# Down's weight sums by DMA into two residual quarters, and whole SwiGLU tiles loaded for its tile sums

## The chip, the cores and the metric

One core of a Trainium2 chip runs the kernel in a single launch. The metric is the device time of one execution in microseconds (us). The kernel before takes 1428.65 us, the median of 3 runs (1428.42 to 1428.69). Line numbers (L121) are those of the kernel before, whose profile is shown.

## The reference

The reference is one layer of a transformer-like encoder in fp32: batch 1, sequence 256, width 2048, SwiGLU width 5632. Four mixers, cross-attention on 256 memory rows, and a SwiGLU block follow each other, each with an RMS norm and a residual sum; a last norm ends it.

```python
x = x + mix @ w_out[l]
x = x + cross_attention(rms_norm(x, norm_g[l, 1]), mem_n, w_xq[l], w_xkv[l], w_xo[l])
x = x + swiglu(rms_norm(x, norm_g[l, 2]), w_gate_up[l], w_down[l])
return rms_norm(x, final_norm_g)

def swiglu(h, w_gate_up, w_down):
    gate, up = jnp.split(h @ w_gate_up, 2, axis=-1)
    return (jax.nn.silu(gate) * up) @ w_down
```

The change concerns the last two matrix products: `gate_up` (256 x 2048 by 2048 x 11264) and `down` (256 x 5632 by 5632 x 2048). They take the time from about 700 us to the end.

## The kernel before

**Products in fp32.** Each operand is split into a rounded high part and a residual low part, and a product is three matmuls with the weights moving: high by high, high by low, low by high (`part`, L472 to L474). The activations lie still, as tiles of 128 rows (k) x 256 (sequence), high and low side by side in 512 columns. A matmul has a 128 x 128 still tile and 512 moving columns.

**The weight stream.** All weights come as slabs of 128 x 2048 fp32 (1 MB) in the order in which the program uses them. `_load` (L105 to L129) issues a slab's DMA on SP's queue into one of three `raw` buffers. `_plain` (L147) turns it into two halves of 1024 columns: ScalarE casts the high part (L166), VectorE subtracts it for the residual (L167). The halves lie in a ring of three pairs of buffers `wh` and `wl`, and pools of stages that have ended are lent to the ring for a while, so a cast waits until TensorE has done with an earlier half.

**Paired slabs.** Two k-tiles and two column blocks together are a 2 x 2 product of blocks. A plain slab ("N" in a plan) takes eight block products, 24 matmuls. A paired slab takes seven by a Strassen-like scheme, 21 matmuls: it needs sums of weight blocks and sums of activation blocks. `_sums` (L171 to L199) makes its four parts of 1024, 512, 1024 and 1024 columns (L178, L179), and the weight sums by VectorE adds of 128 x 512 (L189). `combine` (L477 to L494) makes the activation sums of two tiles, in small adds, and splits them into high and low (L338 and L322). `paired_rows` (L502) walks through a plan, takes the parts as they come, and adds seven products into PSUM banks.

**Where the weight sums come from.** In gate_up a paired slab is "summed": the first sum is made by DMA in a quarter of `res`, the residual rows (four buffers of 128 x 1024, `res0` to `res3`), which are parked in DRAM meanwhile (`leave`). Three slabs ahead (`SUMS`), SP loads 256 KB (L114), ScalarE copies it beside itself (L119), and POOL issues a DMA of 512 KB that adds to what is there (L121). SP then loads only 1536 columns of the slab itself (L124), and VectorE has two adds instead of four. Down's paired slabs are not summed before: all four adds are VectorE's.

**gate_up** (L1100 to L1233) makes 11 blocks of 512 gate and 512 up columns, eight slabs each; blocks 1 to 10 follow the plans in `GROUPS`. A block's result is transposed by VectorE (L598) and stored to DRAM as `hidden` by POOL (`store_turned`, L594). It is loaded back in tiles of 128 x 256 by POOL (`load_turned`, L602, issued at L605) into `tmp` and split by ScalarE and VectorE (`split`, L330 and L322) into the slots `f[k]`, k = 0 to 43 (`fetch`, L1140). 22 of them are fetched during gate_up, the other 22 from the tenth block on, six loads ahead. Slots lie in buffers of earlier stages (`act`, `f`, `z`).

**down** (L1235 to L1310) makes the 2048 columns in two passes of 1024, 22 slabs each, by the plans in `PASSES`; the second pass leaves three slabs to `down_end`. Pair i sums the tiles f[2i] and f[2i+1]; `combine` there first adds the high and low parts of each tile back together (two adds of 128 x 256), since the slots hold nothing else. `mixed` and `done` add the results into `res`, which is reloaded from DRAM in four DMAs of 512 KB right after gate_up (L1230).

**What sets the order.** Every engine runs its queue in program order, and the program is written in TensorE's order. Side work (loads of tiles, `combine`) are generators in `Background` (L243): a planner counts TensorE's time and what VectorE owes, and steps a generator when its yielded pause has passed; `ready` and `before` step it in any case where a tile or sum is needed. `keep` and `keep_place` pin the places of instructions in their engine's queue, and from the end of the attention on the casts and residual splits of the stream keep their order.

Of the kernel before, what the change touches and what calls it, by code (L numbers as in the profile page):

```python
# [24 lines left out]
R = 256  # L25
# [15 lines left out]

LATE = 12

GATE_UP = 1920 // 16 + 8
# [5 lines left out]
PAIRED = {a + i for a, plan in [(GATE_UP + 8 * j, GROUPS[j % len(GROUPS)]) for j in range(10)] + [(DOWN, PASSES[0]), (DOWN + 22, PASSES[1])]  # L50
          for i, x in enumerate(plan) if x in "Ss"}
AHEAD = (-3, -3)

SUMS = [{GATE_UP + 8 * j + i + a: GATE_UP + 8 * j + i for j in range(10) for i, x in enumerate(GROUPS[j % len(GROUPS)]) if x == "S"}
        for a in AHEAD]

SUMMED = {GATE_UP + 8 * j + i for j in range(10) for i, x in enumerate(GROUPS[j % len(GROUPS)]) if x == "S"}

# [18 lines left out]
class Stream:  # L77


    def __init__(self, tc, pools, W, bg):  # L80
# [13 lines left out]
        self.two = []  # L94
        self.begun = []

# [8 lines left out]
    def _load(self, n):  # L105
# [4 lines left out]
        self.raw = slot[0].tile([P, 2048], F32, name="raw", tag="raw")  # L110
        if n // 16 in SUMS[0]:
            t = self.sums[0]
            self.sums.append(self.sums.pop(0))
            nc.sync.dma_start(t[:, 0:512], self.W[SUMS[0][n // 16]][:, 1536:2048])  # L114
            self.begun.append(t)
        if n // 16 in SUMS[1]:
            t = self.begun.pop(0)
            mark = len(nc.cur_bb.bb.instructions)
            nc.scalar.copy(t[:, 512:1024], t[:, 0:512])  # L119
            self.keep(mark)  # L120
            nc.gpsimd.dma_start(t, self.W[SUMS[1][n // 16]][:, 512:1536], accum_op=ALU.add)  # L121
            self.two.append(t)
# [170 lines left out]
class Block:  # L293
# [563 lines left out]
    def whole(self, c):  # L857
        return self.res[c].rearrange("p k r -> p (k r)")

    def leave(self, c):  # L860
        self.nc.sync.dma_start(self.rd[:, c * 1024:(c + 1) * 1024], self.whole(c))
# [238 lines left out]
    def gate_up(self, gp, f, z):  # L1100
# [39 lines left out]
        def fetch(k0, k1, ahead, pause, after=0, slow=False):  # L1140

            m = {}
            for k in range(k0, k1 + ahead):
# [11 lines left out]
                if k >= k0 + ahead:  # L1155
                    while k0 == 0 and k - ahead >= 20 and "free" not in box:
                        yield
# [48 lines left out]
        up(0, ps[1])  # L1206
        early = fetch(0, FT - 22, 2, 2.0, 12, True)
        self.bg.drain(comb)
        for j in range(1, DFF // 512):
            plan = GROUPS[(j - 1) % len(GROUPS)]  # L1210
            if j == 10:
                box["free"] = True
# [22 lines left out]
    def down(self, f, sp):  # L1235
# [8 lines left out]
        u = sp.tile([P, 512], F32, name="u")  # L1244
        sums = [((2 * i, 2 * i + 1), z[i % 8]) for i in range(PASSES[1].count("S"))]
# [41 lines left out]
        def ready(k):  # L1287

            need = min(FT, max(k + 3, FT - 22 + next(asked) * 3 // 4))
            while self.have < need:  # L1290
                self.bg.step(next(e for e in self.bg.q if e[0] is self.fetch))

        for i, plan in enumerate(PASSES):
            n = plan.count("S")
# [13 lines left out]
            if i == 0:  # L1308
# [683 lines left out]
```

## Time and profile before

| What | Value |
|---|---|
| Median of 3 runs | 1428.65 us (1428.42 to 1428.69) |
| Profiled execution | 1428.43 us, span 1426.6 us |
| Mean granted TensorE clock | 0.999 |
| TensorE busy | 1416.5 us, 99% of the span |
| VectorE busy | 1174.3 us, 82% |
| ScalarE busy | 850.2 us, 60% |
| POOL busy | 243.4 us, 17% |
| Moved by DMA | 344.84 MB, 242 GB/s |
| Down starts | about 1186 us |

In the profile, PE is TensorE, DVE is VectorE, ACT is ScalarE, POOL is GpSimd, and SP issues most DMAs. A group's row has the line, the engine, the operation, out<-in with tile names and shapes, the count, the busy time, the mean ns of one, and the idle time before them with what ended it. A timeline's row has the start and duration in us, and in brackets the idle time before it and its releaser. A row of windows has the stretch in us, its length, the busy us (and count) of PE, PE's weight loads, VectorE, ScalarE and POOL, the granted clock, the mean busy share of the DMA engines (a value over 1 comes from overlapping records) and GB/s. A row of DMA issues has the count, KB each, and the median us from issue to landing.

### The profile page before, as it was taken

How to read it: one execution, taken by the hardware profiler on the slowest of the kernel's cores; microseconds unless marked ns; L12 is line 12 of the kernel's file. 1: busy time of each engine (PE TensorE's matmuls, PEld its weight loads, DVE VectorE, ACT ScalarE, POOL GpSimd, SP SyncE). 2: the span in 40 equal slices, each digit the busy share in tenths (PEclk: the TensorE clock that was granted, in tenths of full speed). 3: DMA queues.
4: the chain of work that ended last, by engine and by line, in shares of the span. 5: the costliest groups of instructions: out<-in, count | busy, mean ns of one | idle time of the engine just before them, and what ended most of it. 6: DMA issues, size and time to landing. Idle time of an engine off the chain costs nothing.

```text
span 1426.6 us, 18663 instructions
## 1 busy us (share of the span) xinstructions
PE 1416.5 (99%) x6562; PEld 1176.1 (82%) x6562; DVE 1174.3 (82%) x1782; ACT 850.2 (60%) x1242; POOL 243.4 (17%) x315
## 2 busy tenths in 40 slices
PE   9999999999999999999999999999999999999997
PEld 8888888888888888888888888888888888788886
DVE  6667868787878767677578999999999988989997
ACT  7566665445755555555465676667666665655655
POOL 0000100003212233531331121122211024000000
PEclk9999999999999999999999999999999999999999
DMA  9886554457566797965798999999999898665554
GB/s 356 294 291 250 204 198 174 161 177 232 183 216 215 234 278 249 276 197 188 252 298 257 265 280 283 288 291 260 278 291 273 276 276 242 212 235 179 193 220 148
DMA packets 72462, 344.84 MB, mean 242 GB/s; under 512 B 10894, under 2 KB 12591, under 8 KB 45745
## 3 DMA queue, kind: packets, MB, share of 16 engines
q1 hardware_dynamic: 52976, 285.31, 57.4%
q0 software_dynamic: 18960, 57.69, 17.2%
q8 instruction: 51, 0.84, 0.2%
q10 hardware_dynamic: 432, 0.66, 0.1%
q14 instruction: 43, 0.34, 0.1%
HBM read 321.07 MB, written 22.54 MB: 241 GB/s over the span
## 4 chain that ended last, share of the span: by engine, by line
PE 92%; issue 3%; DVE 2%; DMA 2%; POOL 1%; ACT 0%; SPq 0%; DVEq 0%; ACTq 0%; POOLq 0%
PE pg L472 21%; PE pg L474 21%; PE pg L473 21%; PE pm L473 6%; PE pm L474 6%; PE pm L472 6%; PE pg L420 4%; PE pg L421 2%; PE pm L1445 1%; DMA raw<-in_W 1%; PE pm L1074 1%; DMA tmp<-hidden 1%; POOL tmp L605 1%; PE pm L1045 1%; DVE wl L179 0%
## 5 line engine op out<-in xcount | busy, mean ns | idle before, releaser
L167 DVE TENSOR_TENSOR wl<-raw,wh 128x1024 fp32r<-128x1024 f32 (+1 forms) x395 | 473.7, 1212 | 161.3 <-ACT wh L166 159.4
L166 ACT CAST wh<-raw 128x1024 fp32r<-128x1024 f32 (+1 forms) x395 | 406.4, 1042 | 253.0 <-PE pg L474 189.0
L472 PE MATMUL pg<-wh,act 128*128 128x512 f32 (+1 forms) x1165 | 455.5, 391 | 0.0
L474 PE MATMUL pg<-wh,act 128*128 128x512 f32 (+1 forms) x1165 | 453.9, 390 | 0.5 <-DVE act L322 0.5
L473 PE MATMUL pg<-wl,act 128*128 128x512 f32 (+1 forms) x1165 | 453.6, 389 | 0.2 <-DVE wl L167 0.2
L474 PEld LDWEIGHTS pg<-wh,act 128*128 128x128 f32 x1165 | 218.9, 188 | 47.0 <-DVE act L322 1.1
L472 PEld LDWEIGHTS pg<-wh,act 128*128 128x128 f32 x1165 | 219.0, 188 | 46.8 <-issue 1.5
L473 PEld LDWEIGHTS pg<-wl,act 128*128 128x128 f32 x1165 | 219.0, 188 | 45.1 <-DVE wl L167 0.5
L178 ACT CAST wh<-raw 128x1024 fp32r<-128x1024 f32 (+1 forms) x177 | 161.5, 918 | 158.8 <-DVE raw L189 62.7
L179 DVE TENSOR_TENSOR wl<-raw,wh 128x1024 fp32r<-128x1024 f32 (+1 forms) x177 | 182.7, 1057 | 25.7 <-ACT wh L178 24.3
L473 PE MATMUL pm<-wl,act 128*128 128x512 f32 x290 | 112.9, 389 | 0.2 <-DVE wl L167 0.2
L472 PE MATMUL pm<-wh,act 128*128 128x512 f32 x290 | 112.8, 389 | 0.0
L474 PE MATMUL pm<-wh,act 128*128 128x512 f32 x290 | 112.8, 389 | 0.0
L420 PE MATMUL pg<-act,wh 128*128 128x512 f32 x256 | 90.5, 395 | 0.0
L121 POOL DMA_DIRECT2D res<-in_W x39 | 35.0, 897 | 238.3 <-ACT res L119 211.1
L421 PE MATMUL pg<-act,wl 128*128 128x256 f32 x256 | 71.8, 280 | 0.0
L189 DVE TENSOR_TENSOR raw<-raw 128x512 f32<-128x512 f32 x99 | 68.2, 689 | 1.6
L473 PEld LDWEIGHTS pm<-wl,act 128*128 128x128 f32 x290 | 54.4, 188 | 11.8 <-DVE wl L167 0.5
L474 PEld LDWEIGHTS pm<-wh,act 128*128 128x128 f32 x290 | 54.4, 188 | 11.3
L472 PEld LDWEIGHTS pm<-wh,act 128*128 128x128 f32 x290 | 54.4, 188 | 11.3
L420 PEld LDWEIGHTS pg<-act,wh 128*128 128x128 f32 x256 | 48.1, 188 | 10.5
L178 ACT CAST wh<-res 128x1024 fp32r<-128x1024 f32 x39 | 41.2, 1055 | 14.8 <-PE pg L474 4.1
(376 smaller groups left out, 1933.0 us busy)
## 6 DMA issues: line engine op xcount, KB each, us to landing
raw<-in_W SPq DMA_DIRECT2D x207, 1024.0 KB, 5.5
raw<-in_W SPq DMA_DIRECT2D x39, 768.0 KB, 8.9
res<-in_W POOLq DMA_DIRECT2D x39, 512.0 KB, 9.7
res<-in_W SPq DMA_DIRECT2D x39, 256.0 KB, 4.9
raw<-in_W SPq DMA_DIRECT2D x11, 512.0 KB, 7.1
hidden<-g POOLq DMA_DIRECT2D x22, 256.0 KB, 4.0
tmp<-hidden POOLq DMA_DIRECT2D x44, 128.0 KB, 10.5
features<-tmp POOLq DMA_DIRECT2D x32, 128.0 KB, 4.6
```

Source lines behind the costliest of these rows:

```text
L121: nc.gpsimd.dma_start(t, self.W[SUMS[1][n // 16]][:, 512:1536], accum_op=ALU.add)
L166: nc.scalar.copy(wh[:, a:b], r[:, a:b])
L167: nc.vector.tensor_tensor(out=wl[:, a:b], in0=r[:, a:b], in1=wh[:, a:b].bitcast(F32), op=ALU.subtract)
L178: nc.scalar.copy(wh, src)
L179: nc.vector.tensor_tensor(out=wl, in0=src, in1=wh.bitcast(F32), op=ALU.subtract)
L189: nc.vector.tensor_tensor(out=out, in0=a, in1=b, op=ALU.add)
L420: self.nc.tensor.matmul(p[:, :], wh, slot[:, :], start=start, stop=False)
L421: self.nc.tensor.matmul(p[:, 0:R], wl, slot[:, 0:R], start=False, stop=stop)
L472: self.nc.tensor.matmul(p, hi, wh, start=start, stop=False)
L473: self.nc.tensor.matmul(p, hi, wl, start=False, stop=False)
L474: self.nc.tensor.matmul(p, lo, wh, start=False, stop=stop)
L605: self.nc.gpsimd.dma_start(t.rearrange("p (g t) -> p g t", t=32), src)
```

## The change

- All ten paired blocks of gate_up have the plan "NSSNSSNN"; the tenth was "NSNSNSNN". That is 40 paired slabs instead of 39.
- Down has seven paired slabs in its first pass instead of six, and ten instead of nine in the second. All seven of the first and seven of the second ("S") are now summed by DMA as in gate_up; three ("s") keep the four adds on VectorE.
- Down's sums have only the quarters `res2` and `res3`. `begins` sets at which slab a sum is begun: three slabs ahead, but not before the slab after that of the quarter's last user; the first two are begun six slabs ahead, which is in gate_up. SP's load, ScalarE's copy and POOL's accumulating load are now issued at one place.
- `res0` and `res1` are reloaded after gate_up, `res2` and `res3` in the second pass, two slabs after its last "S".
- `combine` takes, in Down, the whole tiles of a pair from DRAM: POOL loads both (128 KB each) into the two halves of one tile `u`, the generator pauses for 10 us of TensorE's time, and the two adds that joined high and low are left out. The next pair's loads are issued when the adds of the pair before stand in the queue.
- The sums of a pair are forced two slabs ahead of use rather than at the slab itself.
- 20 tiles are fetched during gate_up instead of 22, the rest seven loads ahead instead of six, from the third slab of the last block on instead of the fourth; the rate at which Down asks for them is 5/8 a call instead of 3/4, and more of the first pass's first steps go to the early tiles.

In the built programs, matmuls go from 6450 to 6441, VectorE's two-operand instructions from 1324 to 1301, ScalarE's copies and casts from 956 to 980, SP's DMAs from 371 to 386 and POOL's from 305 to 340.

```diff
-GROUPS = *["NSSNSSNN"] * 9, "NSNSNSNN"
+GROUPS = "NSSNSSNN",
-PASSES = "NNNNNSNNSNNSNSNNSNNSNN", "NSNSNSNSNSNSNSNSNSNNNN"
+PASSES = "NNNNNSNSNNSNSNNSNSNSNN", "NSSNSNSNSNSNSNssNsNNNN"
...
+def begins():
+    at = {}
+    for ns, tiles in (([n for n in sorted(SUMMED) if n < DOWN], 4), ([n for n in sorted(SUMMED) if n >= DOWN], 2)):
+        for i, n in enumerate(ns):
+            a = max(n - 3, ns[i - tiles] + 1) if i >= tiles else n - (3 if tiles > 2 else 6)
+            at[a] = n
+    return at
+SUMS = begins()
...
-    def combine(self, z, a, b):
-        tt, t, u, v, w = self.tt, *(self.tmp() for _ in range(4))
-        for x, y in ((t, a), (u, b)):
-            tt(x, y[:, 0:R].bitcast(F32), y[:, R:512].bitcast(F32), ALU.add)
-        yield SOON
+    def combine(self, z, a, b, whole=None):
+        tt = self.tt
+        if whole:
+            t, u, v, w = *whole, self.tmp(), self.tmp()
+        else:
...
-        early = fetch(0, FT - 22, 2, 2.0, 12, True)
+        early = fetch(0, EARLY, 2, 2.0, 12, True)
...
-                rest = fetch(FT - 22, FT, 6, SOON, slow=True)
+                rest = fetch(EARLY, FT, 7, SOON, slow=True)
...
+                if (j, i) == (10, 4):
+                    self.st.sums = whole[2:]
-                if j == 10 and i > 2:
+                if j == 10 and i > 1:
                     next(rest)
...
-        for c, x in enumerate(whole):
-            nc.sync.dma_start(x, self.rd[:, c * 1024:(c + 1) * 1024])
+        self.fetch_rows((0, 1))
...
         def combined(n):
-            for ks, x in sums[len(made):n]:
-                yield from self.combine(x, *(f[k] for k in ks))
+            whole = [u[:, a:a + R] for a in (0, R)]
+            todo = sums[len(made):n]
+            def load(ks):
+                mark = self.mark()
+                for y, k in zip(whole, ks):
+                    self.load_turned(y, self.ff, k)
+                self.keep_place(mark)
+            load(todo[0][0])
+            yield 10.0
+            for i, (ks, x) in enumerate(todo):
+                yield from self.combine(x, *(f[k] for k in ks), whole)
                 made.append(x)
-                yield 2.0
+                if i + 1 < len(todo):
+                    load(todo[i + 1][0])
+                    yield 10.0
...
-            need = min(FT, max(k + 3, FT - 22 + next(asked) * 3 // 4))
+            need = min(FT, max(k + 3, EARLY + next(asked) * 5 // 8))
...
-            g = self.bg.add(combined(n))
+            g = self.bg.add(combined(n), go=True)
...
-                while plan[j] == "S" and len(made) <= plan[:j].count("S"):
+                while len(made) < sum(x in "Ss" for x in plan[:j + 2]):
                     self.bg.step(next(e for e in self.bg.q if e[0] is g))
+                if i and j == plan.rindex("S") + 2:
+                    self.fetch_rows((2, 3))
...
-                                        () if i else range(2 * n, 2 * n + 8))
+                                        () if i else range(2 * n, EARLY))
```

More of the change, by code (lines that the diff above doesn't have):

```diff
@@ L42 @@
 LATE = 12
+EARLY = 20
 GATE_UP = 1920 // 16 + 8
-GROUPS = *["NSSNSSNN"] * 9, "NSNSNSNN"
+GROUPS = "NSSNSSNN",
 DOWN = GATE_UP + 80
-PASSES = "NNNNNSNNSNNSNSNNSNNSNN", "NSNSNSNSNSNSNSNSNSNNNN"
[L50 to L57, printed above, removed]
+PASSES = "NNNNNSNSNNSNSNNSNSNSNN", "NSSNSNSNSNSNSNssNsNNNN"
+PLANS = [(GATE_UP + 8 * j, GROUPS[j % len(GROUPS)]) for j in range(10)] + [(DOWN, PASSES[0]), (DOWN + 22, PASSES[1])]
+PAIRED, SUMMED = ({a + i for a, plan in PLANS for i, x in enumerate(plan) if x in kinds} for kinds in ("Ss", "S"))
+def begins():
[3 more added lines that the diff above has]
+            a = max(n - 3, ns[i - tiles] + 1) if i >= tiles else n - (3 if tiles > 2 else 6)
+            assert a not in at and a < n, (a, n)
+            at[a] = n
+    return at
+SUMS = begins()
 LAG, OWED, SOON, FAR = 1.3, 0.9, 0.01, 18.0
@@ L110, in _load @@
         self.raw = slot[0].tile([P, 2048], F32, name="raw", tag="raw")
-        if n // 16 in SUMS[0]:
+        if n // 16 in SUMS:
             t = self.sums[0]
             self.sums.append(self.sums.pop(0))
[L114 to L117, printed above, removed]
+            nc.sync.dma_start(t[:, 0:512], self.W[SUMS[n // 16]][:, 1536:2048])
             mark = len(nc.cur_bb.bb.instructions)
@@ L120, in _load @@
             self.keep(mark)
-            nc.gpsimd.dma_start(t, self.W[SUMS[1][n // 16]][:, 512:1536], accum_op=ALU.add)
+            nc.gpsimd.dma_start(t, self.W[SUMS[n // 16]][:, 512:1536], accum_op=ALU.add)
             self.two.append(t)
@@ L475, in part @@
         self.bg.pe(0.68 * wh.shape[1] / 512)
-    def combine(self, z, a, b):
-        tt, t, u, v, w = self.tt, *(self.tmp() for _ in range(4))
-        for x, y in ((t, a), (u, b)):
-            tt(x, y[:, 0:R].bitcast(F32), y[:, R:512].bitcast(F32), ALU.add)
-        yield SOON
+    def combine(self, z, a, b, whole=None):
[3 more added lines that the diff above has]
+        else:
+            t, u, v, w = (self.tmp() for _ in range(4))
+            for x, y in ((t, a), (u, b)):
+                tt(x, y[:, 0:R].bitcast(F32), y[:, R:512].bitcast(F32), ALU.add)
+            yield SOON
         tt(v[:, 0:P], t[:, P:R], u[:, P:R], ALU.subtract)
@@ L858, in whole, with fetch_rows @@
         return self.res[c].rearrange("p k r -> p (k r)")
+    def fetch_rows(self, cs):
+        for c in cs:
+            self.nc.sync.dma_start(self.whole(c), self.rd[:, c * 1024:(c + 1) * 1024])
     def leave(self, c):
@@ L1155, in fetch @@
                 if k >= k0 + ahead:
-                    while k0 == 0 and k - ahead >= 20 and "free" not in box:
-                        yield
                     mark = self.mark()
@@ L1293, in down @@
         for i, plan in enumerate(PASSES):
-            n = plan.count("S")
-            g = self.bg.add(combined(n))
+            n = sum(x in "Ss" for x in plan)
+            g = self.bg.add(combined(n), go=True)
             late = (0, LATE)[i]
```

5 lines of the change are left out of this document (1 added, 4 removed).

## The prediction

> **What bounds the kernel now.** I read the busy shares first, then the stages, then TensorE's own waits. The page:
>
> ```profile
> span 1426.6 us, 18663 instructions
> PE 1416.5 (99%) x6562; PEld 1176.1 (82%) x6562; DVE 1174.3 (82%) x1782; ACT 850.2 (60%) x1242; POOL 243.4 (17%) x315
> ```
>
> PE is busy 99% of the span. The busy time by stage (gate_up's paired blocks, Down's first and second pass, the end):
>
> ```profile
> core 0: us, PE busy (x) PEld busy (x) DVE busy (x) ACT busy (x) POOL busy (x), PEclk, DMA share, GB/s
> 700.00:1186.00 486.00, 486.00 (x2146) 402.43 (x2145) 439.52 (x558) 311.99 (x394) 92.69 (x109) 1.00 0.92 280
> 1186.00:1310.00 124.00, 123.27 (x542) 101.36 (x541) 113.51 (x188) 71.65 (x108) 16.45 (x19) 1.00 0.66 215
> 1310.00:1405.00 95.00, 94.72 (x417) 77.60 (x415) 90.81 (x129) 57.33 (x72) 0.00 (x0) 1.00 0.55 202
> ```
>
> PE is without a gap in gate_up and idle for 1.0 us in both passes of Down, at full granted clock. All that PE waited for from 700 us on, in us, times and longest:
>
> ```profile
> PE pg L474 <- DVE act L322: 0.5, 1, 0.5
> PE pm L472 <- ACT y L338: 0.2, 1, 0.2
> PE pm L473 <- DVE wl L167: 0.2, 1, 0.2
> ```
>
> So each matmul less is worth its own time, and VectorE, though 92% busy in Down's first pass (113.51 of 124), holds PE up for under 1 us. Two places in PE's timeline give the price of a matmul and the two stalls:
>
> ```profile
> 1208.18 0.39 PE L472 MATMUL pg<-wh,z 128*128 128x512 f32 x1
> 1213.62 0.39 PE L472 MATMUL pm<-wh,act 128*128 128x512 f32 x1
> 1215.71 0.47 PE L472 MATMUL pm<-wh,y 128*128 128x512 f32 x1 [0.25 <-ACT y L338]
> 1232.33 0.50 PE L474 MATMUL pg<-wh,act 128*128 128x512 f32 x1 [0.48 <-DVE act L322]
> ```
>
> 1208.18 and 1213.62 are the starts of Down's slabs 4 (plain) and 5 (paired): 24 matmuls in 5.44 us, so 0.227 each, a paired slab of 21 takes 4.76, and Down starts at 1213.62 - 5 x 5.44 = 1186.42.
>
> **The change part by part.** *Removed on PE:* the built kernel has 9 matmuls of 128x512 less (one paired slab more in gate_up and one in each pass, 3 matmuls each): 9 x 0.227 = 2.04 us, all on the path. If the two stalls of 0.25 and 0.48 go too, 2.77. The profiled execution took 1428.43 us (span 1426.6 and 1.8 around it; 0.2 under the median of 1428.65), so 1425.66 is the floor of this change, unless something outside Down moves too.
>
> *Removed on VectorE:* two adds in each of 14 slabs that become summed, and two adds of whole tiles in each of 17 pairs of Down:
>
> ```profile
> L189 DVE TENSOR_TENSOR raw<-raw 128x512 f32<-128x512 f32 x60 | 41.2, 687 | 0.5
> L322 DVE TENSOR_TENSOR tmp<-f 128x256 f32<-128x256 f32 x10 | 4.2, 418 | 0.0
> L322 DVE TENSOR_TENSOR tmp<-tmp 128x128 f32<-128x128 f32 x36 | 9.6, 285 | 0.1
> L179 DVE TENSOR_TENSOR wl<-raw,wh 128x1024 fp32r<-128x1024 f32 x45 | 54.9, 1220 | 6.5 <-ACT wh L178 6.3
> L179 DVE TENSOR_TENSOR wl<-raw,wh 128x512 fp32r<-128x512 f32 x15 | 10.3, 686 | 1.1 <-ACT wh L178 1.1
> ```
>
> That is about 14 x 2 x 0.687 = 19.2 us and 17 x 2 x 0.42 = 14.3 us of an engine for which PE waits under 1 us: worth at most the stalls counted above. If VectorE becomes the bound after a late input, the relief only shortens the recovery.
>
> *Added:* 14 sums by DMA in Down (a load by SP, a copy by ScalarE, an accumulating load by POOL), and two loads of 128 KB per pair by POOL into one tile `u`. Rows of such transfers, with median us to landing, and ScalarE's and POOL's price of issuing:
>
> ```profile
> res<-in_W POOLq DMA_DIRECT2D x39, 512.0 KB, 9.7
> res<-in_W SPq DMA_DIRECT2D x39, 256.0 KB, 4.9
> tmp<-hidden POOLq DMA_DIRECT2D x44, 128.0 KB, 10.5
> L119 ACT COPY res<-res 128x512 f32<-128x512 f32 x39 | 23.9, 614 | 0.0
> L121 POOL DMA_DIRECT2D res<-in_W x39 | 35.0, 897 | 238.3 <-ACT res L119 211.1
> L166 ACT CAST wh<-raw 128x1024 fp32r<-128x1024 f32 x140 | 142.2, 1047 | 30.6 <-PE pg L474 14.2 <-PE pm L474 13.8 <-issue 2.2
> ```
>
> ScalarE's copies (14 x 0.61) fit beside the 58 to 60% of its use in Down (71.65 of 124, 57.33 of 95); POOL has idle time. What can cost are the loads' landings: `u` is one buffer, so a pair's loads can only be issued when the pair before has read it, and the adds that read `u` stand in VectorE's queue in front of the residual splits that PE needs next.
>
> *T1, the first paired slab of Down.* `u` lies where gate_up's last tiles lie, so its first loads wait until the last block's two stores have landed:
>
> ```profile
> 1189.69 1.52 POOL L600 DMA_DIRECT2D hidden<-g  x2 [33.32 <-DVE g L598]
> 1191.20 7.03 POOL L605 DMA_DIRECT2D tmp<-hidden  x8
> 1206.21 1.91 POOL L605 DMA_DIRECT2D tmp<-hidden  x2 [0.36 <-issue]
> hidden<-g POOLq DMA_DIRECT2D x2, 256.0 KB, 4.2
> L605 POOL DMA_DIRECT2D tmp<-hidden x1: 882/882/882, 1207.2 to 1207.2; - x1
> DMA to landing us min/median/max: 11.5/11.5/11.5
> DMA to landing us min/median/max: 5.2/10.7/13.1
> 1195.00:1200.00 5.00, 5.00 (x23) 4.13 (x23) 2.11 (x4) 2.49 (x4) 4.33 (x6) 1.00 1.06 254
> ```
>
> The row with two numbers after x1 is one load: issued at 1207.2, landed 11.5 later; it is the fifteenth from 1191.2 on. The last landing row is that of all 22 loads of this burst. DMA is full there (share 1.06).
>
> In after Down starts 0.68 earlier, at 1185.74; the second store starts at 1190.4 - 0.7 and lands 4.2 later, at 1193.9. POOL then issues, at 0.88 each (7.03 / 8), two loads into `u`, eleven of tiles, and the second pair's two: these are fourteenth and fifteenth, and the last starts at 1206.2 or later. I take 1206.4 and the burst's median of 10.7 to landing rather than 11.5, since 1 MB of residual rows is no longer reloaded at this place: 1217.1. Four adds of 0.285 and the 512-wide split of 0.69 follow: 1218.9. Slab 5 begins at 1185.74 + 5 x 5.44 = 1212.94 and needs that split two products later, at 1214.30: **4.6 late**. VectorE then has 4.4 us of work up to the sum's split (two adds 1.37, splits and tiles 1.83, 1.22), while PE has one product of 0.68: **3.7 more**. T1 = 8.3. If these loads landed in the least time of the row below (4.9), 0; with 13.1, 10.7.
>
> *T2 to T5, later pairs.* The DMA share falls after 1220, and so would the landing:
>
> ```profile
> DMA to landing us min/median/max: 4.9/10.0/13.7
> raw<-in_W SPq DMA_DIRECT2D x21, 1024.0 KB, 6.5
> raw<-in_W SPq DMA_DIRECT2D x29, 1024.0 KB, 5.0
> ```
>
> The first is that of the 22 tile loads between 760 and 1150; the weight loads took 6.5 between 1100 and 1240 and 5.0 between 1250 and 1400, a factor of 0.77. A load alone on its queue (4.9) would take 3.8, the median 7.7 (or 10.0 unchanged); I take L = 6.3, midway between 4.9 and 7.7.
>
> T2: the adds of the fourth pair stand in VectorE ahead of the tile split that slab 9's last step needs. From the end of slab 7 (T): a cast 1.05, a split 1.22, two tile splits 0.84, three adds that free `u` 0.86, POOL's second load starts at T + 4.85, lands at + L; an add, a 512-wide split and the tile's 0.42 make 1.39. Needed at T + 5.44 + 3 x 1.36 + 0.45 = T + 9.97. Late by L - 3.7: **2.6** (0 to 4.5).
>
> T3 to T5: here POOL issues the pair's loads behind the accumulating load of a sum, which waits for its quarter. From the start T of a plain slab ahead of a summed one: half of it 2.72, the cast 1.05 and the split 1.22 that free the quarter: T + 5.0; SP's 256 KB 3.8 (4.9 x 0.77), the copy 0.61, POOL's issue 0.9, its second load starts at T + 11.2. Slab 12's fourth part is needed at T + 5.44 + 4.76 + 5.44 + 3.40 = T + 19.04, with 1.14 of adds and 1.22 of split before it: late by L - 5.5, **0.8** (0 to 2.7). For slab 17 of the first pass and slab 10 of the second it is the third part, T + 17.68, behind three adds and 1.22: late by L - 4.4, **1.9** each (0 to 3.8). The other pairs come out 1 to 3 us early.
>
> Sum: 8.3 + 2.6 + 0.8 + 1.9 + 1.9 = 15.5, from 0 to 25.5. **1425.66 + 15.5 = 1441.2.** Between ends so far apart I take the value nearest to the row of the same transfer in the same burst, for T1 half of the whole.
>
> The Trainium skill ("DMA: Bandwidth & Descriptors", Anatomy of one DMA — SWDGE (gpsimd) path) fits a POOL-issued transfer as 2.0 us plus bytes over 436 GB/s: for 128 KB an estimate of 2.3 us. By that no load here is late and the time is that of rival B. The trace's same loads take 4.9 at best and 10.0 in the middle, so the measurement speaks against it here.
>
> *Moved, at no cost:* two early tiles go from gate_up to Down's burst (counted among the eleven). Residual quarters 2 and 3 are reloaded in the second pass instead of at 1186 (512 KB each), about three slabs, 15 us, ahead of their use; if a raw load queued behind them on SP came late, ScalarE's cast would wait, and SP's queue fills 56% of the DMA engines there:
>
> ```profile
> q1 hardware_dynamic: 4236, 30.90, 56.1%
> ```
>
> Down's first two sums begin in gate_up, in quarters that gate_up has left; SP's 256 KB pass beside a queue in which PE lost nothing.
>
> **The rivals.** *B: all loads are covered.* If the loads land in about 5 us throughout, T1 to T5 vanish and the time is 1425.7. For it: the minimum of 4.9 and a quarter less DMA traffic late in Down; against it: 11.5 in the very burst. *C: only one later stall stays* (T1 covered, since the tile loads ahead of it are not held, and T2 and T3 as computed): 1425.7 + 3.4 = 1429.1, no change. *R2: two quarters are too few* (slower, by another mechanism). From the start of the second pass, the quarter of its first sum is free at T + 5.0 and the third sum lands 3.8 + 0.6 + 0.9 + 9.7 later, at T + 20.0; its slab begins at T + 20.4, and its sum's split, behind two adds, is needed at T + 22.44, so the sum by T + 19.85. It decides from the median landing on: before's accumulating loads took up to 14.0 us.
>
> ```profile
> DMA to landing us min/median/max: 5.8/9.7/14.0
> ```
>
> At 14.0 PE waits 4.5 there, beside the forecast's waits: 1445.7. Further on a quarter comes round every two paired and two plain slabs, 20.4, and the chain has 1 us to spare even at 14.0. Before hides it with four quarters.
>
> **How the numbers follow.** Forecast (T1 with at least one other): 0.57, 1441.2, its own range 1431.5 to 1450. B: 0.26, 1425.7. C: 0.07, 1429.1. R2: 0.10, 1445.7. About 0.2% (2.9 us) is what a measurement of this kernel can tell from no change, so faster means under 1425.8, which the floor just reaches: half of B, 0.13. The other half and C are the same, 0.20. Slower: 0.57 + 0.10 = 0.67. The range is 1425.5 to 1450: it takes in B, C and R2 and leaves out the ends at which all five landings are the longest.
>
> **What would show it.** PE's waits should name the splits of VectorE behind adds that read `u`, idle 5 to 10 us between 1214 and 1225 (T1), and 1 to 3 us in slabs 9, 12, 17 and in the second pass's slab 10; VectorE there should wait for POOL's loads into `u`, landing 9 to 12 us after issue in the burst and 5 to 8 later. PE should have 9 matmuls less. If PE shows no gap near 1214, the landing or POOL's issue was overestimated, and B or C holds; if it waits for sums in the quarters, it is R2. If PE's loss lies in gate_up, where one more sum is made, all five terms are of the wrong place.

## The result and the profile after

The changed kernel takes 1465.71 us, the median of 4 runs (1465.06 to 1466.28), beside 1428.67 (1428.42 to 1429.41) for the kernel before on the same chip: 37.0 us more, ratio 1.0258 with a 95% interval of 1.0241 to 1.0276. The direction was forecast; the forecast of 1441.2 and its range up to 1450 fell short. The busy shares of the changed kernel (its lines are numbered a little higher: L184, L327 and L614 are the L179, L322 and L605 of before):

```profile
span 1464.5 us, 18795 instructions
PE 1430.1 (98%) x6553; PEld 1180.7 (81%) x6553; DVE 1165.5 (80%) x1759; ACT 860.8 (59%) x1266; POOL 275.1 (19%) x350
```

TensorE has 9 matmuls less and yet is busy 13.6 us longer (1430.1 beside 1416.5), so what it did took 15.6 us more than 9 x 0.227 less would give; and it is idle for 34.4 us of the span instead of 10.1, 24.3 more. Both parts together, 24.3 + 13.6, are the 37.9 that the two spans differ by. The stages show where, and the column ahead of the last two (PEclk) shows most of why the busy time grew:

```profile
700.00:1186.00 486.00, 486.00 (x2146) 402.56 (x2145) 440.90 (x560) 314.98 (x397) 94.66 (x111) 1.00 0.93 279
1186.00:1230.00 44.00, 37.44 (x148) 29.56 (x147) 30.50 (x52) 20.79 (x36) 19.32 (x23) 0.88 0.84 228
1230.00:1270.00 40.00, 36.42 (x150) 28.55 (x148) 26.86 (x46) 20.90 (x34) 9.78 (x11) 0.96 0.83 230
1270.00:1310.00 40.00, 31.79 (x119) 24.65 (x120) 26.02 (x42) 19.13 (x28) 5.48 (x6) 0.89 0.60 171
1310.00:1350.00 40.00, 39.97 (x174) 32.64 (x173) 35.55 (x51) 25.02 (x37) 4.54 (x5) 0.98 0.80 244
1350.00:1400.00 50.00, 44.96 (x185) 35.69 (x184) 35.40 (x48) 25.45 (x32) 7.08 (x8) 0.93 0.85 244
```

gate_up is untouched. In Down the granted clock is 0.88 to 0.98 in every stretch. The trace has it at half in five stretches (1219.2 to 1229.5, 1246.5 to 1250.0, 1273.8 to 1277.3, 1304.5 to 1311.4 and 1389.8 to 1396.8). PE's 65 matmuls there took 26.75 us of busy time, 12.0 more than 65 x 0.227. The rest of the 15.6 us is no half clock; the first matmuls behind a wait also come a little late. What PE waited for from 700 us on (total, times, longest):

```profile
PE pm L478 <- DVE wl L184: 10.6, 4, 3.8
PE pg L478 <- DVE wl L184: 9.2, 2, 4.8
PE pg L479 <- DVE act L327: 1.7, 2, 0.9
PE pg L477 <- ACT act L335: 1.2, 1, 1.2
PE pm L477 <- ACT wh L183: 0.7, 1, 0.7
PE pm L478 <- DVE wl L172: 0.5, 1, 0.5
```

That is 23.9 us, 19.8 of it on residual splits of paired slabs (L184). What VectorE waited for most between 1186 and 1400, and one such place, at Down's first paired slab:

```profile
DVE tmp L327 <- DMA u<-hidden: 26.3, 6, 6.1
```

```profile
1211.36 0.41 DVE L327 TENSOR_TENSOR act<-tmp,act 128x256 fp32r<-128x256 f32 x1
1217.92 0.49 DVE L327 TENSOR_TENSOR tmp<-u 128x128 f32<-128x128 f32 x2 [6.14 <-DMA u<-hidden]
...
1218.86 0.68 DVE L184 TENSOR_TENSOR wl<-raw,wh 128x512 fp32r<-128x512 f32 x1
```

VectorE stands at an add on `u` until a load lands, with the split that TensorE needs queued behind. It did so six times. And this is what TensorE did after the wait at slab 17:

```profile
1305.20 0.79 PE L478 MATMUL pm<-wl,y 128*128 128x512 f32 x1 [3.78 <-DVE wl L184]
1305.79 0.63 PE L479 MATMUL pm<-wh,y 128*128 128x512 f32 x1
1306.22 0.63 PE L477 MATMUL pm<-wh,y 128*128 128x512 f32 x1
```

From start to start the matmuls take 0.43 us (1305.79 to 1306.22) instead of 0.23, until 1311.4, 6 us after the wait.

### The profile page after: what moved, and what is told of

It reads as the page before. It is cut to its first block, busy times and chain, and to the rows that moved or that the text cites. A ratio compares the mean times of both kernels' runs of the same rounds, so it can differ in the third digit from the quotient of the medians.

```text
span 1464.5 us, 18795 instructions
## 1 busy us (share of the span) xinstructions
PE 1430.1 (98%) x6553; PEld 1180.7 (81%) x6553; DVE 1165.5 (80%) x1759; ACT 860.8 (59%) x1266; POOL 275.1 (19%) x350
## 4 chain that ended last, share of the span: by engine, by line
PE 88%; DMA 6%; DVE 3%; issue 1%; ACT 1%; POOL 1%; SPq 0%; ACTq 0%; DVEq 0%; POOLq 0%
PE pg L478 20%; PE pg L479 20%; PE pg L477 20%; PE pm L478 6%; PE pm L479 6%; PE pm L477 6%; PE pg L425 4%; DMA u<-hidden 3%; DMA res<-in_W 2%; PE pg L426 2%; DVE wl L184 1%; PE pm L1472 1%; PE pm L1088 1%; DVE raw L194 1%; ACT wh L183 1%
## 5 line engine op out<-in xcount | busy, mean ns | idle before, releaser
L172 DVE TENSOR_TENSOR wl<-raw,wh 128x1024 fp32r<-128x1024 f32 (+1 forms) x389 | 467.2, 1212 | 171.4 <-ACT wh L171 169.4
L171 ACT CAST wh<-raw 128x1024 fp32r<-128x1024 f32 (+1 forms) x389 | 400.2, 1041 | 245.3 <-PE pg L479 182.2
L183 ACT CAST wh<-raw 128x1024 fp32r<-128x1024 f32 (+1 forms) x174 | 156.2, 907 | 140.0 <-DVE raw L194 51.0
L184 DVE TENSOR_TENSOR wl<-raw,wh 128x1024 fp32r<-128x1024 f32 (+1 forms) x174 | 177.2, 1045 | 32.8 <-ACT wh L183 31.3
L126 POOL DMA_DIRECT2D res<-in_W x54 | 48.3, 895 | 394.7 <-ACT res L124 336.8
L477 PE MATMUL pm<-wh,act 128*128 128x512 f32 x284 | 110.7, 390 | 0.0
L479 PE MATMUL pm<-wh,act 128*128 128x512 f32 x284 | 110.5, 389 | 0.0
L183 ACT CAST wh<-res 128x1024 fp32r<-128x1024 f32 x54 | 56.9, 1054 | 26.5 <-PE pg L479 10.5
L184 DVE TENSOR_TENSOR wl<-res,wh 128x1024 fp32r<-128x1024 f32 x54 | 65.6, 1215 | 3.4 <-ACT wh L183 3.4
L479 PEld LDWEIGHTS pm<-wh,act 128*128 128x128 f32 x284 | 53.3, 188 | 10.9
```

The costliest lines, as they stand in the source:

```text
L126: nc.gpsimd.dma_start(t, self.W[SUMS[n // 16]][:, 512:1536], accum_op=ALU.add)
L171: nc.scalar.copy(wh[:, a:b], r[:, a:b])
L172: nc.vector.tensor_tensor(out=wl[:, a:b], in0=r[:, a:b], in1=wh[:, a:b].bitcast(F32), op=ALU.subtract)
L183: nc.scalar.copy(wh, src)
L184: nc.vector.tensor_tensor(out=wl, in0=src, in1=wh.bitcast(F32), op=ALU.subtract)
L477: self.nc.tensor.matmul(p, hi, wh, start=start, stop=False)
```

## The experiments

Times stand beside those of the kernel before on the same chip: 1429.22 for e1 to e4, 1428.95 for e5 to e8, 1429.08 for e9 to e12. In the diffs, `...` stands for lines left out.

**The loads taken out** (e1_adds_back: VectorE joins high and low parts again; the sums by DMA stay).

```diff
-            load(todo[0][0])
-            yield 10.0
             for i, (ks, x) in enumerate(todo):
-                yield from self.combine(x, *(f[k] for k in ks), whole)
+                yield from self.combine(x, *(f[k] for k in ks))
                 made.append(x)
-                if i + 1 < len(todo):
-                    load(todo[i + 1][0])
-                    yield 10.0
+                yield 2.0
```

> The changed kernel, but the tile sums are made as before from high and low parts on VectorE, with no load into u; plans, the sums by DMA and the two quarters stay. Theory U (the loss comes from loads into the single buffer u, whose adds stand in VectorE's queue ahead of residual splits, with the slower TensorE clock that follows each long stall): PE's waits on splits behind u go, and with them the slow clock; 1425.7 to 1431 us, 14.3 us more work on VectorE being hidden. Rival R2 (two quarters are too few, the chain of accumulating loads sets the pace): the waits stay, over 1445.

Measured: 1433.35 (8 runs, 1431.72 to 1435.64), ratio 1.0029 (1.0018 to 1.0040). PE's waits fell from 23.9 to 5.6 us; the longest row:

```profile
PE pg L478 <- DVE wl L184: 2.3, 3, 1.1
```

So without the loads into `u` 32.4 of the 37.0 us are gone, although VectorE then has 20 adds of 128x256 more to do, some 8 us (20 x 0.42). The 14.3 us of the expectation counted 17 pairs; the sums made in the first pass serve the second too, so there are ten. The median lies 2 us above the top of what was expected: sums by DMA in Down, alone, do not pay either. ScalarE stands at its copy until SP's 256 KB have landed, with casts behind it, as it does in the changed kernel (16.5 us in seven waits):

```profile
ACT res L124 <- DMA res<-in_W: 13.9, 6, 3.6
```

**Two buffers for the whole tiles** (e2_two_u) in the first pass: `res0` takes every other pair and is reloaded at the pass's last paired slab.

```diff
-        self.fetch_rows((0, 1))
+        self.fetch_rows((1,))
...
-            whole = [u[:, a:a + R] for a in (0, R)]
+            wholes = [[x[:, a:a + R] for a in (0, R)] for x in ((u, u) if made else (u, self.whole(0)))]
...
-            load(todo[0][0])
+            ahead = 1 if made else 2
+            for i in range(ahead):
+                load(i)
...
```

> The changed kernel with two buffers for the whole tiles in Down's first pass: the residual quarter res0, reloaded only at the first pass's last paired slab, takes every other pair, and a pair's loads are issued one pair earlier. The second pass keeps one buffer. Theory U: the stalls of slabs 5, 12, 15 and 17 go, that of the second pass's slab 10 (4.4 us and 2.9 of slow clock) stays: 1432 to 1438 us. If POOL's in-order queue is the cause rather than the single buffer (loads wait behind accumulating loads), stalls of 3 us or more stay in the first pass too: over 1445.

Measured: 1452.50 (2 runs), ratio 1.0164 (1.0143 to 1.0184). The expectation that the single buffer alone is the cause fell. The first paired slab is mended (three waits of 0.4 to 1.1 us for 4.8 and 1.8) and slab 17's stall is gone, but slabs 12 and 15 still stall (3.88 and 1.65 us): POOL issues in order, and the loads stand behind an accumulating load that waits for ScalarE's copy into its quarter. POOL and VectorE before slab 12:

```profile
1252.71 0.91 POOL L126 DMA_DIRECT2D res<-in_W  x1 [8.48 <-ACT res L124]
1253.30 2.15 POOL L614 DMA_DIRECT2D res<-hidden  x2
```

```profile
1263.86 0.49 DVE L327 TENSOR_TENSOR tmp<-res 128x128 f32<-128x128 f32 x2 [4.75 <-DMA res<-hidden]
```

**The loads without the sums** (e3_before_whole): the kernel before, with its plans, and only `combine`, the loads and the earlier forcing of pairs of the changed kernel.

```diff
-            for ks, x in sums[len(made):n]:
-                yield from self.combine(x, *(f[k] for k in ks))
+            load(todo[0][0])
+            yield 10.0
+            for i, (ks, x) in enumerate(todo):
+                yield from self.combine(x, *(f[k] for k in ks), whole)
...
```

> The kernel before with only the loads of whole tiles into u and the earlier forcing of pairs: plans and adds of weight sums on VectorE as before, no accumulating load in Down. Theory U with landing times set by the accumulating loads ahead (4.8 to 5.5 us alone, 8 to 9.9 behind one): only the first paired slab stalls, 6 to 7 us and some 3 to 4 of slow clock: 1436 to 1441. If u alone is enough whatever is on POOL: as many stalls as in the changed kernel, 1450 to 1470. If u is harmless without the sums: 1428.

Measured: 1438.46 (2 runs), ratio 1.0066 (1.0045 to 1.0086). As expected with landings set by the accumulating loads: one long stall, at the first paired slab, and slow matmuls behind it.

```profile
1223.42 0.79 PE L473 MATMUL pm<-wl,y 128*128 128x512 f32 x1 [6.86 <-DVE wl L179]
1224.01 0.63 PE L474 MATMUL pm<-wh,y 128*128 128x512 f32 x1
```

All 18 loads into `u` (nine pairs), min, median and max to landing:

```profile
DMA to landing us min/median/max: 2.7/3.3/9.1
```

The 9.1 is that of the burst at Down's start; the later ones took 2.7 to 6.1. In the changed kernel the loads after 1225 took

```profile
DMA to landing us min/median/max: 3.6/7.6/9.9
```

and those issued right behind an accumulating load 9.5, 9.4, 8.9, 6.3 and 7.9 at the least. Loads alone cost 9.2 us, sums alone (e1_adds_back, with more pairs) 4.1; together 37. Most of the loss is what they do to each other.

**The idle time filled** (e4_filler): 82 matmuls by a tile of zeros behind the first matmul of six stalled products.

```diff
+FILL = {(5, 2): 20, (5, 3): 8, (12, 5): 15, (15, 3): 5, (17, 3): 16, (32, 3): 18}
...
         self.nc.tensor.matmul(p, hi, wh, start=start, stop=False)
+        for _ in range(fill):
+            self.nc.tensor.matmul(p, self.nil, wh, start=False, stop=False)
...
```

> The changed kernel with 82 more matmuls by a tile of zeros (they add nothing to the result) at six places, each right where TensorE stalled, as many as fit into the measured stall (20, 8, 15, 5, 16, 18; 18.6 us at full clock). Theory: the half clock after a stall comes from the idle time itself, so with the idle time filled the clock stays up and 8 to 12 us are saved by doing more work: 1453 to 1458. Rival (the slow matmuls come from something else, such as memory traffic by the late DMAs): no gain, 1465 to 1475.

Measured: 1466.96 (2 runs), ratio 1.0265 (1.0244 to 1.0286). The clock did what the theory says where the fill covered the stall:

```profile
1186.00:1230.00 44.00, 42.33 (x184) 33.92 (x183) 29.50 (x52) 20.94 (x37) 18.36 (x22) 1.00 0.82 222
```

The clock is 1.00 for 0.88 in this first stretch. But nothing was saved: the loads come no earlier. POOL's issues for one pair, here and then in the changed kernel:

```profile
1275.42 2.15 POOL L618 DMA_DIRECT2D u<-hidden  x2
1275.29 2.15 POOL L614 DMA_DIRECT2D u<-hidden  x2
```

PE at full clock reached the next wait sooner and waited there longer: it began slab 8 at 1237.15 instead of 1239.00, waited in it for 2.65 us instead of 1.19, and began slab 9 at 1247.39, beside 1247.28. Slab 13 and the slab behind the second pass's stall begin at the same time, too (1274.41 beside 1274.38, 1396.43 beside 1396.40). So the late splits, and through them the loads, set the pace here, not TensorE; the half clock fills time that would mostly have been idle. The two columns of the account above (24.3 idle, 15.6 slow) are therefore not two causes that can be taken away one by one.

**The loads on ScalarE's queue** (e5_u_scalar) from the second pair on.

```diff
...
-                    self.load_turned(y, self.ff, k)
+                    self.load_turned(y, self.ff, k, nc.scalar if made else nc.gpsimd)
```

> The changed kernel, with the loads into u issued by ScalarE from the second pair on, right behind the casts of the pair before, which wait for the same adds; so they no longer stand behind the accumulating loads in POOL's queue. Still one buffer. Theory P (POOL's order makes the loads late: 8 to 10 us and a wait for the sum's quarter): the stalls of slabs 12, 15, 17 and of the second pass's slab 10 go or fall under 1.5 us each; T1 stays; 1440 to 1450. Rival B1 (one buffer is too few by itself: the pair before must have been read first): stalls as before, 1460 or more.

Measured: 1462.47 (2 runs), ratio 1.0234 (1.0212 to 1.0256): theory P fell. Slab 17's stall went, but slabs 5, 12 and 15 wait 7.6, 5.4 and 2.4 us, and a slab of the second pass 4.1. With one buffer the loads cannot be issued until the pair before is read, on whatever queue, and beside an accumulating load they still took up to 10.4 us. The 12 loads up to 1310:

```profile
DMA to landing us min/median/max: 2.5/5.7/10.4
```

The 16 DMA engines are shared: the Trainium skill ("DMA: Bandwidth & Descriptors", Queues, rings and completion order) has each engine take turns between the queues packet by packet. The landings of 10.4 on this queue, beside an accumulating load of POOL's, agree; what share of the turns such a load gets, no run here shows.

**Both cures** (e9_two_u_scalar): two buffers, loads issued by ScalarE (the two edits together).

> Two buffers for the whole tiles in Down's first pass, as in e2_two_u, and the loads issued by ScalarE, as in e5_u_scalar: neither a buffer in use nor POOL's queue delays their issue in the first pass. Theory (issue is what is late; each cure alone left the other cause): no wait of VectorE for a whole tile in the first pass, only the second pass's stall stays; 1436 to 1446. Rival (the loads take 10 us whenever an accumulating load runs beside them, so nothing helps but leaving one of the two out): stalls of over 2 us stay in slabs 12 to 17, 1450 or more.

Measured: 1447.73 (2 runs), ratio 1.0130 (1.0111 to 1.0148), 1.7 above what the first theory gave. Slabs 12, 15 and 17 no longer stall, as it said: in the first pass VectorE waits for a whole tile only 0.4 us. What PE waits for most is now at casts of ScalarE, 3.0 us at the first paired slab and 3.6 in the second pass:

```profile
PE pm L477 <- ACT wh L183: 3.7, 2, 3.0
PE pg L477 <- ACT wh L183: 3.6, 1, 3.6
```

In the first place ScalarE was held for 3.2 us in issuing one of the loads, with a cast behind it. The second is the stall that was to stay, now at slab 8 of the second pass: with the one buffer of the second pass VectorE waits for a load into `u`, and the cast stands in ScalarE's queue behind one that waits for VectorE. The issue, and VectorE's wait from 1310 to 1400:

```profile
1214.33 3.16 ACTq L614 DMA_DIRECT2D res<-hidden  x1
```

```profile
DVE tmp L327 <- DMA u<-hidden: 4.0, 1, 4.0
```

So two things made the loads of slabs 12 and 15 late, the buffer and POOL's order, and each cure alone left the other; for slab 17 either was enough.

**The clock by itself** (e8_delays): the kernel before, with five residual splits in gate_up done over again.

```diff
+MORE = {2 * (GATE_UP + 8 * j + 3): k for j, k in ((0, 3), (2, 4), (4, 5), (6, 6), (8, 8))}
...
-            nc.vector.tensor_tensor(out=wl[:, a:b], in0=r[:, a:b], in1=wh[:, a:b].bitcast(F32), op=ALU.subtract)
+            for _ in range(MORE.get(n // 8, 1)):
+                nc.vector.tensor_tensor(out=wl[:, a:b], in0=r[:, a:b], in1=wh[:, a:b].bitcast(F32), op=ALU.subtract)
```

> The kernel before with five residual splits of gate_up done over again 2, 3, 4, 5 and 7 times more (1.2 us each, same result), in blocks 1, 3, 5, 7 and 9, so that TensorE waits a graded time in a stage where it otherwise never waits. Theory (a long wait brings half clock for about 5 us, whatever its cause): no slow matmuls after waits under about 1.5 us, 2 to 3 us of extra time after each wait over 3; the time is 1428.7 plus the waits plus 2 to 3 for each long one. Rival (slow matmuls belong to Down and its memory traffic): matmuls stay at full rate, the time is 1428.7 plus the waits.

Measured: 1450.18 (2 runs), ratio 1.0148 (1.0126 to 1.0169). The five places made PE wait 0.25, 0.5, 1.8, 3.0 and 5.4 us. The last one, and the clock around the third, fourth and fifth:

```profile
1138.50 0.79 PE L475 MATMUL pg<-wl,act 128*128 128x512 f32 x1 [5.35 <-DVE wl L169]
1139.09 0.63 PE L476 MATMUL pg<-wh,act 128*128 128x512 f32 x1
1139.52 0.63 PE L475 MATMUL pg<-wl,act 128*128 128x512 f32 x1
...
1142.38 0.40 PE L476 MATMUL pg<-wh,act 128*128 128x512 f32 x1
```

```profile
955.00:985.00 30.00, 27.99 (x121) 22.23 (x120) 28.98 (x32) 19.46 (x24) 3.55 (x4) 1.00 0.83 246
1040.00:1060.00 20.00, 16.74 (x66) 13.04 (x65) 18.38 (x21) 8.50 (x11) 0.00 (x0) 0.91 0.75 244
1130.00:1150.00 20.00, 14.42 (x55) 11.14 (x54) 18.04 (x19) 5.37 (x8) 0.00 (x0) 0.83 0.50 183
```

No slow matmul after waits of up to 1.8 us; nine after 3.0 and nine after 5.4, at 0.43 from start to start instead of 0.23, 1.7 and 1.8 us in all: somewhat less than the 2 to 3 expected. So the half clock comes from the wait, in gate_up as in Down. The Trainium skill ("TensorE: Matmul & The Clock Gate", Part 1: The HAM clock gate) says it: half clock after an idle window of about 3.4 us, full clock after a busy one. The nine slow matmuls, 3.9 us from 1138.50, agree. Between 700 and 1186 PE did 2064 matmuls, 82 fewer than the kernel before, which are 18.6 us; the five waits (10.9) and the slow matmuls (3.5) are 14.4 of it, and the other 4 us were not traced. They put the time above the theory's own sum, too (1428.7, 10.9 and 4 to 6, about 1445).

A wait need not be that long: in e2_two_u one of 1.65 us, at slab 15, brought half clock, too:

```profile
1284.57 0.80 PE L478 MATMUL pm<-wl,y 128*128 128x512 f32 x1 [1.65 <-DVE wl L184]
1285.16 0.63 PE L479 MATMUL pm<-wh,y 128*128 128x512 f32 x1
```

So did two waits of 1.19 and 0.74 us close together in slab 8 of the changed kernel, while single waits of 1.44 (its slab 15) and 1.8 us (here) did not. Every wait of 2.2 us or more in these runs did.

**The plans alone** (e6_plans_only): the kernel before with 40, 7 and 10 pairs, all sums in Down on VectorE.

```diff
-GROUPS = *["NSSNSSNN"] * 9, "NSNSNSNN"
+GROUPS = "NSSNSSNN",
...
-PASSES = "NNNNNSNNSNNSNSNNSNNSNN", "NSNSNSNSNSNSNSNSNSNNNN"
+PASSES = "NNNNNSNSNNSNSNNSNSNSNN", "NSSNSNSNSNSNSNSSNSNNNN"
```

> The kernel before with the changed kernel's plans alone (40, 7 and 10 pairs: 9 matmuls less); in Down all weight sums and tile sums are VectorE's as before. If VectorE has room for two more pairs: 1426 to 1427.5, the 2.0 us of matmuls. If VectorE is the bound as soon as pairs are added (two pairs are some 9 us of VectorE's time): 1429 to 1436 with PE waiting for splits in Down's first pass.

Measured: 1432.08 (10 runs), ratio 1.0024 (1.0014 to 1.0034): VectorE has no room for two more pairs in Down. It is busy 119.3 us from 1186 to 1310 and 92.1 from 1310 to 1405, 96 and 97% (113.5 and 90.8 before). PE waits three times on casts of paired slabs, and ScalarE's casts from 1310 to 1400 wait for VectorE's adds of weight blocks more often than in the kernel before (18.1 us, ten times, 2.9 at most):

```profile
PE pm L472 <- ACT wh L178: 2.0, 2, 1.0
PE pg L472 <- ACT wh L178: 0.6, 1, 0.6
```

```profile
ACT wh L178 <- DVE raw L189: 21.2, 13, 3.3
```

**The fortieth pair alone** (e11_gate_up_only: `GROUPS` as changed, the rest as before).

> The kernel before with only the fortieth pair in gate_up: 3 matmuls less, 0.68 us, in a stage where TensorE does not wait: 1427.9 to 1428.4 beside 1428.7 to 1429.0, inside what can be told. Rival: the fourth sum of the last block is late, with a wait there of over 1 us: 1429 to 1431.

Measured: 1429.07 (11 runs), ratio 0.9998 (0.9989 to 1.0007): no difference that can be told. The block's end moves forward against the blocks ahead of it by 0.7 us, the 0.68 of its three matmuls (VectorE's transposes of the last blocks start 0.92 later than in the kernel before at 1106.9, and 0.22 later at 1148.41).

**No copy** (e7_no_copy): the first experiment, with ScalarE's copy replaced by a second load by SP, in gate_up too.

```diff
-            nc.scalar.copy(t[:, 512:1024], t[:, 0:512])
+            nc.sync.dma_start(t[:, 512:1024], self.W[SUMS[n // 16]][:, 1536:2048])
```

> The changed kernel with VectorE's adds of high and low parts instead of loads into u, and with ScalarE's copy of 256 KB replaced by a second load of the same columns by SP (in gate_up too). Theory C (what is left of the loss without u is ScalarE standing at that copy until SP's load has landed, casts queued behind it): the waits on tiles and on splits in the second pass go, 1426 to 1429. Rival (the accumulating loads ahead of tile loads on POOL, or VectorE's load): 1431 to 1436, as with the copy.

Measured: 1444.98 (4 runs), ratio 1.0111 (1.0095 to 1.0127), 11.6 over the version with the copy. 40 more loads of 256 KB in gate_up, whose DMA share was 0.93, make weights late there: VectorE's transposes start 1.23 later than in the kernel before at 779.18, and 9.96 later at 1148.41. ScalarE's wait for slabs between 700 and 1186, which the kernel before does not have among its longest:

```profile
ACT wh L169 <- DMA raw<-in_W: 33.4, 11, 4.4
```

In Down PE still waits 5.4 us on tiles, casts and splits (5.6 with the copy), so the copy is not shown to be what is left of the loss there; the extra traffic spoils the comparison.

**Sums by DMA in the second pass alone** (e10_sums_second), no loads into `u`, the first pass as before.

```diff
-PASSES = "NNNNNSNSNNSNSNNSNSNSNN", "NSSNSNSNSNSNSNssNsNNNN"
+PASSES = "NNNNNsNNsNNsNsNNsNNsNN", "NSSNSNSNSNSNSNssNsNNNN"
...
```

> The changed kernel without loads into u, with the first pass's plan as before (six pairs, adds by VectorE) and the second as changed (seven sums by DMA and three on VectorE). If what is left in e1_adds_back lies in the first pass (tile loads behind accumulating loads on POOL, ScalarE at the copy): 1426 to 1428.5. If two quarters are too few in the second pass, too (waits on splits around its second to fourth paired slab): 1429 to 1433.

Measured: 1430.92 (10 runs), ratio 1.0018 (1.0008 to 1.0027). PE waits 0.4 us in the first pass and 0.9 after it, on one cast and one split; neither VectorE nor ScalarE's casts wait for a late sum in the second pass. So two quarters suffice there, although the time lies in the range that was given for too few: it is 1.8 us over the kernel before, where 6 matmuls less should have saved 1.4. The loss is in the second pass, where PE does 406 matmuls in 95 us and the kernel before 417; the 11 are 2.5 us:

```profile
1310.00:1405.00 95.00, 93.97 (x406) 74.87 (x405) 87.61 (x128) 59.10 (x77) 4.22 (x5) 1.00 0.75 238
```

The waits name only 0.9 of it; the rest is in matmuls that come too little late to show as idle time, and what makes them late this run does not settle.

**The loads with all pairs and no sum by DMA in Down** (e12_whole_no_sums), two buffers in the first pass.

```diff
-PASSES = "NNNNNSNSNNSNSNNSNSNSNN", "NSSNSNSNSNSNSNssNsNNNN"
+PASSES = "NNNNNsNsNNsNsNNsNsNsNN", "NssNsNsNsNsNsNssNsNNNN"
...
```

> All pairs of the changed kernel (40, 7 and 10) with the whole tiles loaded, two buffers in the first pass, and no sum by DMA in Down: all its weight sums are VectorE's. Theory (the loads and the accumulating loads disturb each other; without the latter a load lands in 3 to 6 us, and 14 us less of tile adds give VectorE the room that e6_plans_only lacked): 1426 to 1429, no stall over 1.5 us. Rival (the burst of tiles at Down's start makes the second pair late even with two buffers): one stall of 4 us or more at the first paired slab, with slow clock: 1433 to 1440.

Measured: 1434.03 (5 runs), ratio 1.0036 (1.0023 to 1.0048). VectorE never waits for a whole tile, and the 14 loads into `u` land in

```profile
DMA to landing us min/median/max: 2.7/3.9/7.3
```

That half of the theory holds, and the time is 18.5 us under that of e2_two_u, which has the same two buffers and the sums by DMA. But it is 5 us over the theory's top: at the first paired slab ScalarE and VectorE come late by 1.6 and 1.4 us with 2 us of slow matmuls, and PE waits some 2 us more on later casts. No version tried here beats the kernel before.

## Why the prediction was wrong

The places and the waits were right: adds on `u` in VectorE's order ahead of the splits, loads late, at slabs 5, 9, 12, 17 and the second pass's slab 10. Two steps failed: the time to landing that the later terms rest on, and a sum that counts a late split at its lateness alone.

- **The sum had no term for TensorE's clock after a wait.** It priced a late split at its lateness. Every wait of 2.2 us or more brought half clock (e8_delays: 1.7 to 1.8 us lost each time; in the changed kernel 12.0 of the 15.6 us by which PE's busy time grew against its matmuls). The trace of the kernel before could not price it: its clock falls only behind PE's last matmul, when nothing is left to be slowed.

```profile
1405.00:1419.00 14.00, 13.78 (x60) 11.12 (x60) 11.09 (x25) 6.74 (x15) 0.00 (x0) 1.00 0.17 69
1419.00:1427.00 8.00, 0.00 (x0) 0.00 (x0) 1.84 (x6) 2.15 (x5) 0.00 (x0) 0.76 0.68 245
```

  e4_filler adds that this term cannot simply be added either: where a load sets the pace, the slow matmuls take the place of idle time. There PE waited 11.9 us and was given up to 18.6 us of fills, so with the clock held up the lateness itself comes to more than the 23.9 us below.
- **T1**, 8.3 forecast: 4.76 + 1.79 = 6.55 measured, the first part within 0.2 of the 4.6. That is two errors that cancel: the second pair's last load was issued at 1209.7 instead of 1206.4, and landed after 8.1 instead of 10.7. It was issued late because the 4.2 of the forecast is the median of the last block's two stores, and the later one counts: it started at 1191.3, landed after 5.2 us at 1196.6 and not at 1193.9, and the first loads into `u` began at 1197.2. The two stores of the changed kernel:

```profile
DMA to landing us min/median/max: 3.7/4.5/5.2
```

- **T2**, 2.6 forecast at slab 9's last step: 0.94 there, and 1.19 + 0.74 a slab earlier, on a tile whose load stood behind an accumulating load and a pair's two loads (9.6 to 10.0 to landing) and whose cast stood behind ScalarE's copy (3.71 of waiting for SP's load). I had counted the copies at nothing beside ScalarE's 60%; what hides a copy's 0.61 us does not hide its wait for SP's load.
- **T3 to T5 failed in L.** The forecast took a landing of 6.3, from weight loads that took 0.77 of their time once the burst was over. Behind an accumulating load the later of two loads took 9.4 (slab 12), 9.2 (slab 15), 7.4 (slab 17) and 8.0 (second pass). With these, L - 5.5 and L - 4.4 give 3.9, 3.0 and 3.6; measured 3.56, 3.78 and 4.43, against 0.8, 1.9 and 1.9 forecast. Slab 15, put down as 1 to 3 us early, lost 1.44. The falling DMA share that the 0.77 stood for was that of the kernel before; the change fills it again (0.84 and 0.83 up to 1270, 0.80 and 0.85 from 1310 on). But the share is not all of it: from 1270 to 1310 it is 0.60, and the loads behind an accumulating load took 6.3 to 9.2 there. Without sums by DMA the loads after the burst took 2.7 to 6.1 (e3_before_whole).
- **The relief of VectorE was worth nothing**, as forecast, and 9 matmuls are 2.0 us, of which 0.7 were seen in gate_up. Its size was off, to no effect on the sum: Down sums nine pairs before, not 17, so the whole tiles' adds that went are 18 x 0.42 = 7.6 us and not 14.3.
- **R2** did not come: there is no wait of PE on the second pass's third sum, and e10_sums_second has none. **B** failed by the landings, **C** with it. The estimate of 2.3 us for such a load from the fit in the Trainium skill ("DMA: Bandwidth & Descriptors", Anatomy of one DMA — SWDGE (gpsimd) path) is near the quietest loads (2.7 to 2.9 in e3_before_whole), and a third to a quarter of those that decide.

The idle sum was 15.5 forecast and 23.9 measured; PE's slower matmuls are 15.6 more, and 2.0 go off for the nine that are gone. What stays open: how much of the 37 would be left if the clock alone were held up throughout, since e4_filler filled six places, a wait of 1.2 us grew to 2.6 and a new one of 2.9 opened; and why the sums by DMA alone (e1_adds_back, e10_sums_second) end 2 to 4 us over the kernel before with so little waiting shown.

## What to carry to other kernels

A wait on the bounding engine is not priced by its length alone: look at the granted clock behind waits in a run that has them, and carry a second term for it as an upper bound, since slow work that ends before the next input comes costs nothing. A transfer's time to landing belongs to what else moves at that moment; when a change adds two kinds of transfer that are triggered by the same event, price each beside the other, not by the traffic that was there before. And a load that is issued late for two reasons (a buffer, an order of issue) shows no cure when only one is removed.

## What the runs showed of the hardware

The same load of 128 KB landed in 2.7 to 2.9 us in quiet stretches (e3_before_whole) and in up to 10.4 beside an accumulating load, on POOL's queue (e2_two_u) and on ScalarE's (e5_u_scalar) alike. TensorE went to half clock after every wait of 2.2 us or more, after some of 1.65 to 1.8 and not after others. A DMA that ScalarE issued held it once for 3.2 us (e9_two_u_scalar), so an issue that is moved to another engine can hold that engine up; what held this one, the trace does not name. And 40 additional loads of 256 KB cost nearly 10 us in a stage whose DMA engines were busy 0.93 of the time, though its TensorE had never waited (e7_no_copy).
